# Spreading the output projection, keeping h resident and moving relays and weight loads between engines in a four-layer streaming trunk

## The chip, the cores and the metric

The kernel runs on all 8 cores of one Trainium2 chip (two dies: cores 0 to 3 and 4 to 7). Each core does the same program on its own part of the batch, so there is no traffic between cores. The time is device microseconds of the slowest core. Executions come in two states: in the fast one all cores are granted about the same clock of the tensor engine (0.961 to 0.968 in a run of the changed kernel that took 4025.31 us), in the slow one a die, at times both, has a lower clock for a part of the run (0.84 on die 0 and 0.97 on die 1 in one that took 4400.8).

Engine names in the profile: PE is the tensor engine (PEld its weight loads), DVE is VectorE, ACT is ScalarE, POOL is GpSimd, SP is SyncE, which issues most transfers. In its lines `ps` is a tile of PSUM, the memory that matmuls write to, and `arena` the kernel's buffers in on-chip memory; `hd` (the normalised h), `wq` (weights converted to bf16), `wst` (weights as given) and `yd` (the convolution's result) lie in the chip's main memory.

## The reference

Four gated layers, `x <- x + W_out(mixer(branch) * silu(z))`, and a last RMS norm. The mixers are a causal pooling, a depthwise convolution of width 31 with GLU and LayerNorm, a gated MLP over chunks of 128 positions, and the pooling again.

```python
for i in range(DEPTH):                       # 0 pool, 1 conv, 2 sgu, 3 pool
    h = rmsnorm(x, norm_g[i])                # D_MODEL 1024, D_INNER 2048
    if kind == 0:
        u, z = split(h @ pool_in_w[j]);      y, st = pool_mixer(u, ...)      # windows 2/4/8/16
    elif kind == 1:
        a, gl, z = split(h @ conv_in_w[j]);  y, st = conv_mixer(a * sigmoid(gl), ...)   # then LayerNorm, silu
    else:
        u, v, z = split(h @ sgu_in_w[j]);    y, st = sgu_mixer(u, v, ...)    # W_s @ layernorm(v), times u
    x = x + (y * silu(z)) @ out_w
return rmsnorm(x, final_g), states
```

A core has 4096 prompt positions (8 groups of 512 columns) and one small group of 128 columns (samples), nine groups in all.

## The kernel before

The kernel records operations and lets a scheduler of its own order each engine's queue by simulated times. A queue then runs in that order: in the trace of before each engine does its operations in one and the same order on all 8 cores (3551 on VectorE, 1662 transfers on SyncE), though their times differ. The program has five stages: A the first pooling layer, B the convolution's front (input products, GLU, transposition, a Toeplitz product called a fill, which reads the transposed GLU result of a channel tile, T), C its back (LayerNorm, gate, projection), D the gated MLP, E the second pooling layer.

The output projection of a group is one block: eight steps of sixteen matmuls (L696 in the profile of before). Each step is followed by a residual add on VectorE, a Square on ScalarE and, two *ticks* later, a statistic matmul that sums the squares for the next RMS norm. A tick is one product of eight matmuls or one projection step.

```python
def tick(self):
    for p in self.pend:
        p[0] -= 1
    while self.pend and self.pend[0][0] <= 0:
        self.pend.pop(0)[1]()

def sq_stat(self, xt, k, T, st):
    q = self.sqp.tile()
    self.S.add("act", lambda e: e.activation(out=q..., in_=xt[k]..., func=AF.Square), ...)
    def stat():                                        # run later, after n ticks
        self.pe(lambda e: e.matmul(st[0]..., lhsT=self.ones_d, rhs=q...), ...)
    return stat

def outproj(self, lay, g, ym, wn):
    xt = self.load_x(g, ...)                           # the group's residual, eight tiles
    for m in range(8):
        w = self.chunk(wn(m))
        ...                                            # 16 matmuls
        S.add("dve", ... op=ALU.add ...)               # residual
        S.add("sp", ... store to xs ...)
        self.later(2, self.sq_stat(xt, m, T, st))
        self.tick()
    def fin(): ...                                     # root, reciprocal, eight products, store of h
    self.later(2, fin)

def pool_layer(self, j, lay):
    ...
    for g in range(g0, NG):
        self.pool_cts(j, g, h, range(0, 2), ym)        # a channel tile: two input products, window sums
        self.pending_out()                             # the whole projection of the last group
        self.pool_cts(j, g, h, range(2, 8), ym)
        ...
    self.ulast(j); self.pending_out()
```

In the convolution's front every channel tile goes through the nine groups, forwards and backwards in turn. A tile's fills come between the next tile's products, and the first fill needs all nine parts of T.

```python
for ct in range(16):
    for i in range(NG):
        if not plan[ct * NG + i]:
            hres[g] = self.load_h(g, self.hB)          # 7 of the 9 h tiles stay, the others are loaded again
        pg = self.inproj(w, 128, h, n);  # ACT: sigmoid
        pa = self.inproj(w, 0, h, n);    # DVE: product into G
        S.add("dve", lambda e: e.transpose(T...[strided by NBLK], G...))   # L1028
        for _ in range(2 if i in (2, 4) else 1):
            if fills: fills.pop(0)()                   # 6 Toeplitz matmuls, a PSUM copy on ACT
```

In stage C the gate product `y * silu(z)` runs on GpSimd (L1154). In stage D a group has four chunks of LayerNormed v, then sixteen gating steps; the whole projection of the last group stood between the two.

## Time and profile before

Fast executions took 4175.99 and 4195.81 us; 4583.94 was slow.

I cut each core's trace at the same four events: the first GLU product (A to B), the end of the last fill (B to C), the first v matmul (C to D), the first copy of the last layer's u (D to E). The "floor" is the number of matmuls of each width (512, 136, 128 and fewer columns) by 0.2192, 0.073 and 0.06 us, the rates that the prediction derives: 49 matmuls of 512 columns in 10.74 us, twelve of 136 in 0.88, and the last an estimate from these two. I count it on the cores whose traces hold all 18681 matmuls; on two of the eight some 350 records are missing. These marks differ by up to 43 us from the windows in the prediction. Means over the 8 cores, in us:

| stage | length | floor | above the floor | PE idle |
|---|---|---|---|---|
| A | 980 | 768 | 212 | 181 |
| B | 611 | 536 | 75 | 71 |
| C | 760 | 569 | 191 | 162 |
| D | 1008 | 976 | 32 | 38 |
| E | 806 | 716 | 90 | 77 |
| sum | 4164 | 3564 | 600 | 529 |

(In D PE's matmuls ran 5 us under these rates in all, so the idle time is more than what is above the floor.)

The lines of the profile that carry this are in the prediction below. Here are only stages B and D on the slowest core with these marks; the columns are window, length, busy us of PE, PEld, DVE, ACT, POOL with instruction counts, granted clock, DMA share, GB/s:

```profile
1002.00:1609.00 607.00, 535.90 (x3252) 281.93 (x3316) 524.58 (x450) 318.69 (x566) 29.31 (x66) 0.95 0.75 206
2368.00:3373.00 1005.00, 964.24 (x5028) 467.13 (x5122) 515.63 (x849) 320.94 (x457) 0.20 (x1) 0.99 0.61 198
```

In B VectorE is nearly as full as PE (525 and 536 of 607 us); in D PE is all but gapless.

### The profile page before, as it was taken

The numbers are of one execution on the slowest core, as the hardware profiler recorded it, in microseconds if no ns is written. First come the engines' busy times: TensorE is split into PE (matmuls) and PEld (weight loads), VectorE is DVE, ScalarE is ACT, GpSimd is POOL, SyncE is SP. The second block draws the span as 40 slices with busy tenths as digits, with TensorE's granted clock in tenths as the row PEclk, the third lists the DMA queues.
The fourth block names the chain that finished last, engine by engine and source line by source line (L and its number), as shares of the span: only waits on it lengthen the run. The fifth ranks groups of instructions, "written<-read, shape, count | busy, mean of one in ns | idle before, by whom it ended". The sixth has DMA issues, their size and how long they took to land.

```text
span 4179.6 us, 58691 instructions; the slowest of 8 cores (4148.8 to 4179.6 us)
## 1 busy us (share of the span) xinstructions
PE 3614.8 (86%) x18339; PEld 1720.5 (41%) x18681; DVE 2568.2 (61%) x3551; ACT 1608.5 (38%) x2677; POOL 504.9 (12%) x887
## 2 busy tenths in 40 slices
PE   6996888884997997797886799999999989999996
PEld 2442333342444543243333444444444444444443
DVE  4855677663888995554544445555455666677775
ACT  3332333222554553565565433223333222332222
POOL 1211111111000000224223100000000011111100
PEclk9998999997999998898998899999999999999998
DMA  7655666579886668566656735666556763233224
GB/s 163 127 124 122 139 150 138 135 161 203 203 209 180 187 186 241 176 214 212 221 179 203 239 133 185 197 201 194 194 178 194 246 221 106 91 106 106 94 87 96
DMA packets 274912, 704.49 MB, mean 169 GB/s; under 512 B 53848, under 2 KB 67288, under 8 KB 261296
## 3 DMA queue, kind: packets, MB, share of 16 engines
q1 hardware_dynamic: 257584, 612.62, 45.7%
q0 software_dynamic: 17024, 88.09, 13.3%
q8 instruction: 157, 2.57, 0.3%
q14 instruction: 147, 1.20, 0.1%
HBM read 645.97 MB, written 176.26 MB: 197 GB/s over the span
## 4 chain that ended last, share of the span: by engine, by line
PE 63%; DVE 16%; DMA 8%; issue 6%; ACT 3%; POOL 2%; SPq 1%; DVEq 0%; ACTq 0%; POOLq 0%
PE ps L608 31%; PE ps L696 21%; DVE arena L833 6%; PE ps L1243 5%; DMA arena<-wq 3%; DVE arena L654 3%; DMA arena<-wst 2%; DVE arena L647 2%; DVE arena L843 2%; PE ps L638 2%; POOL arena L1154 2%; DVE arena L1146 1%; DMA yd<-arena 1%; PE ps L1067 1%; PE ps L747 1%
## 5 line engine op out<-in xcount | busy, mean ns | idle before, releaser
L608 PE MATMUL ps<-arena 128*128 128x512 bf16 (+1 forms) x10151 | 2144.7, 366 | 192.3 <-DMA arena<-wq 54.6
L608 PEld LDWEIGHTS ps<-arena 128*128 128x128 bf16 x10368 | 970.5, 99 | 1241.5 <-issue 240.6
L696 PE MATMUL ps<-arena 128*128 128x512 bf16 (+1 forms) x4526 | 1001.0, 374 | 186.3 <-POOL arena L1154 106.5
L696 PEld LDWEIGHTS ps<-arena 128*128 128x128 bf16 x4608 | 443.7, 101 | 700.1 <-issue 253.9
L700 DVE TENSOR_TENSOR arena<-ps,arena 128x512 f32<-128x512 f32 (+1 forms) x288 | 185.3, 646 | 773.2 <-PE ps L696 706.1
L833 DVE TENSOR_TENSOR arena<-arena 128x526 f32<-128x526 f32 (+4 forms) x720 | 476.1, 661 | 105.6 <-ACT arena L811 58.5
L632 ACT ACTIVATE arena<-arena 128x512 bf16<-128x512 f32 (+1 forms) x360 | 208.1, 591 | 749.9 <-DVE arena L700 716.0
L1028 DVE STREAM_TRANSPOSE arena<-arena 128x512 bf16<-128x512 bf16 (+1 forms) x144 | 334.2, 2321 | 11.1 <-DVE arena L1002 0.5
L811 ACT ACTIVATE arena<-ps 128x512 f32<-128x512 f32 x256 | 152.6, 596 | 408.4 <-DVE arena L843 190.2
L1154 POOL TENSOR_TENSOR arena<-arena 128x512 bf16<-128x512 f32 (+1 forms) x144 | 212.0, 1510 | 467.8 <-ACT arena L1148 467.8
L849 ACT ACTIVATE arena<-ps 128x512 f32<-128x512 f32 (+1 forms) x288 | 161.5, 561 | 223.7 <-PE ps L608 202.4
L647 DVE RECIPROCAL arena<-arena 128x512 f32<-128x512 f32 (+1 forms) x54 | 166.5, 3083 | 131.5 <-ACT arena L644 131.5
L858 DVE SCALAR_TENSOR_TENSOR arena<-arena 128x512 bf16<-128x512 f32 (+1 forms) x288 | 204.3, 709 | 48.7 <-DVE arena L843 40.7
L1243 PE MATMUL ps<-arena 128*128 128x512 bf16 x1035 | 228.6, 379 | 4.4 <-DMA arena<-wq 3.2
L814 POOL COPY arena<-arena 128x15 f32<-128x15 f32 x224 | 116.0, 518 | 953.4 <-ACT arena L811 953.1
L654 DVE SCALAR_TENSOR_TENSOR arena<-arena 128x512 bf16<-128x512 f32 (+3 forms) x360 | 226.7, 702 | 5.3 <-DVE arena L647 1.6
L1327 ACT ACTIVATE arena<-ps 128x512 f32<-128x512 f32 (+1 forms) x144 | 80.7, 562 | 377.2 <-PE ps L608 377.0
L809 POOL COPY arena<-arena 128x15 f32<-128x15 f32 x256 | 63.1, 247 | 1260.3 <-DMA o_sgu<-arena 864.7
L843 DVE SCALAR_TENSOR_TENSOR arena<-arena 128x512 f32<-128x512 f32 (+1 forms) x288 | 187.0, 649 | 32.7 <-DVE arena L833 0.5
L1330 DVE TENSOR_TENSOR arena<-ps,arena 128x512 f32<-128x512 f32 (+1 forms) x144 | 92.9, 645 | 171.7 <-PE ps L608 138.8
L1080 DVE STREAM_TRANSPOSE arena<-arena 128x512 f32<-128x512 f32 x144 | 146.5, 1049 | 32.6 <-DMA yd<-arena 32.5
L982 ACT ACTIVATE arena<-arena 32x512 bf16<-32x512 f32 x256 | 160.7, 628 | 13.5 <-PE ps L1067 5.2
(75 smaller groups left out, 2405.2 us busy)
## 6 DMA issues: line engine op xcount, KB each, us to landing
arena<-wq SPq DMA_DIRECT2D x474, 512.0 KB, 4.3
arena<-hd SPq DMA_DIRECT2D x70, 1024.0 KB, 8.1
arena<-wst POOLq DMA_DIRECT2D x104, 512.0 KB, 12.0
xs<-arena SPq DMA_DIRECT2D x192, 256.0 KB, 3.9
arena<-xs SPq DMA_DIRECT2D x192, 256.0 KB, 6.6
arena<-xin SPq DMA_DIRECT2D x128, 256.0 KB, 9.6
wq<-wst POOLq DMA_DIRECT2D x64, 512.0 KB, 10.7
yd<-arena SPq DMA_DIRECT2D x128, 256.0 KB, 5.3
```

Source lines behind the costliest of these rows:

```text
L608: r = e.matmul(P[:, 0:T], lhsT=W[:, k * 256 + base:k * 256 + base + 128], rhs=H[:, k * 512:k * 512 + T], start=(k == 0), stop=(k == 7))
L632: self.S.add("act", lambda e: e.activation(out=q.ap(BF16)[:, 0:T], in_=xt[k].ap()[:, 0:T], func=AF.Square), reads=[xt[k]], writes=[q], cos ...
L647: self.S.add("dve", lambda e: e.reciprocal(out=r.ap()[:, 0:T], in_=r.ap()[:, 0:T]), reads=[r], writes=[r], cost=(6.5 * T + 80) / 1000)
L654: self.S.add("dve", lambda e, k=k: e.scalar_tensor_tensor(out=(h.ap(BF16)[:, k * 512:k * 512 + T] if h is not None else xt[k].ap()[:, 0:T] ...
L696: r = e.matmul(P[:, 0:T], lhsT=W[:, k * 128:(k + 1) * 128], rhs=ym[k].ap(BF16)[:, 0:T], start=(k == 0), stop=(k == 15))
L700: S.add("dve", lambda e, t=t, m=m: e.tensor_tensor(out=xt[m].ap()[:, 0:T], in0=t.ap()[:, 0:T], in1=xt[m].ap()[:, 0:T], op=ALU.add), reads= ...
L833: return e.tensor_tensor(out=V(dst, lo, n), in0=V(src, lo, n), in1=V(src, lo - step, n), op=ALU.add)
L843: S.add("dve", lambda e, u=u, src=src, w=w: e.scalar_tensor_tensor(out=V(src, 15, nt), in0=V(src, 15, nt), scalar=1.0 / w, in1=V(u, 15, nt ...
L858: return e.scalar_tensor_tensor(out=a, in0=b, scalar=self.par[:, P_PSCALE + j * 16 + ct:P_PSCALE + j * 16 + ct + 1], in1=c, op0=ALU.mult, ...
L1028: S.add("dve", lambda e, G=G, T=T, b0=b0, nb=nb: e.transpose(T.ap(BF16)[:, 0:32 * NBLK].rearrange("p (c b) -> p b c", b=NBLK)[:, b0:b0 + n ...
L1154: S.add("pool", lambda e: e.tensor_tensor(out=o.ap(BF16)[:, 0:T], in0=y.ap()[:, 0:T], in1=z.ap()[:, 0:T], op=ALU.mult), reads=[y, z], writ ...
L1243: r = e.matmul(pv.ap()[:, 0:512], lhsT=H[:, k * 512 + c * 128:k * 512 + c * 128 + 128], rhs=w[k // 4].ap(BF16)[:, (k % 4) * 512:(k % 4) * ...
```

## The change

Its intent: take PE's waits away. The block projection becomes a generator of eight steps, pulled one at a time between the next group's input products. The front's transpositions become contiguous; the strided access moves to a second copy on ScalarE, called the relay, for one, and to the copy out of PSUM for the other. All nine h tiles stay resident, for which the second buffer of the convolution's result (Y1) goes. The gate product moves from GpSimd to VectorE. Loads of converted weights go to the Pool queue (GpSimd's), and two more sets are kept converted. The diff is shortened; `...` marks cuts.

```diff
+        yield                                   # outproj is now a generator
         for m in range(8):
+            xt += self.load_x(g, ..., [m])
 ...
             self.later(2, self.sq_stat(xt, m, T, st))
             self.tick()
+            if m < 7:
+                yield
@@ pool_layer
+            pulls = (4, 5, 7, 8, 10, 11, 13, 14)
             self.pool_cts(j, g, h, range(0, 2), ym)
-            self.pending_out()
-            self.pool_cts(j, g, h, range(2, 8), ym)
 ...
+            self.pool_cts(j, g, h, range(2, 16), ym, pulls=pulls)
+            self.add_out(lay, g, ym, wn)
-        self.ulast(j)
-        self.pending_out()
@@ pool_cts, between the z product and its silu
+            if ct in pulls:
+                self.pull()
@@ conv_front
-            if not hit and len(res) > 6:
+            if not hit and len(res) > 9:
 ...
-                S.add("dve", lambda e, ...: e.transpose(T...[strided], G...))
+                t1 = self.t1.tile()
+                S.add("dve", lambda e, ...: e.transpose(t1..., G...))
+                S.add("act", lambda e, ...: e.activation(out=T...[strided], in_=t1..., func=AF.Copy))
@@ buffers of the front
-        self.hB = Pool(S, "hB", 8192, offs(b, 8192, 3) + offs(R + 84 * kb, 8192, 4))
+        self.hB = Pool(S, "hB", 8192, ... 3) + (... 4) + offs(R + 41 * kb, 8192, 2))
-        self.Y1 = Pool(S, "Y1", 17408, offs(R + 24 * kb, 17408, 2))
+        self.Y1 = Pool(S, "Y1", 17408, offs(R + 24 * kb, 17408, 1))
@@ conv_back, gate product
-        S.add("pool", ... op=ALU.mult ...)
+        S.add("dve", ... op=ALU.mult ...)
@@ sgu_layer, after each v product
+                    if q % 2 == 1 and c >= 0:
+                        self.pull(1 if nch > 1 else 4)
-            self.pending_out()                   # stood between the chunks and the gating
@@ load_chunk
-            S.add("sp", ... dma_start(out=t, in_=wq) ..., cost=0.06)
+            S.add("pool", ... dma_start(out=t, in_=wq) ..., cost=0.55)
```

Cut: the last-row products of u moved from stage A into B, precasts (conversions of weights ahead of their use) moved, the projection in stage C pulled after channel tiles 1 to 8, pools and the scheduler's transfer model.

## The prediction

> **What bounds the kernel now.** I read the page first: TensorE (PE) is busy for 86% of the span, VectorE 61%, ScalarE 38%, GpSimd 12%, and the granted clock is below full in many slices.
>
> ```profile
> span 4179.6 us, 58691 instructions; the slowest of 8 cores (4148.8 to 4179.6 us)
> PE 3614.8 (86%) x18339; PEld 1720.5 (41%) x18681; DVE 2568.2 (61%) x3551; ACT 1608.5 (38%) x2677; POOL 504.9 (12%) x887
> ```
>
> The lines' first and last starts cut the span into the five layer stages: A first pooling layer (0 to 985), B convolution front (to 1648), C convolution back with LayerNorm (to 2357), D gating layer (to 3330), E second pooling layer. Second view, engines by stage; columns: window, length, busy us of PE, weight loads, VectorE, ScalarE, GpSimd, clock, DMA share, GB/s.
>
> ```profile
> 0.00:985.00 985.00, 786.42 (x3729) 360.22 (x3798) 626.01 (x927) 297.88 (x516) 160.65 (x396) 0.91 0.66 141
> 985.00:1648.00 663.00, 563.12 (x3383) 294.65 (x3446) 542.49 (x475) 333.43 (x590) 32.09 (x71) 0.93 0.77 206
> 1648.00:2357.00 709.00, 564.52 (x2589) 251.88 (x2641) 334.47 (x465) 420.16 (x714) 215.02 (x150) 0.89 0.61 197
> 2357.00:3330.00 973.00, 947.36 (x4808) 452.45 (x4901) 497.15 (x800) 316.99 (x442) 0.87 (x3) 0.99 0.60 195
> 3330.00:4180.00 850.00, 753.38 (x3842) 361.32 (x3903) 568.07 (x885) 240.00 (x417) 96.24 (x268) 0.95 0.36 117
> ```
>
> Third, a PE floor. The chain in order of time has unbroken runs such as 49 matmuls of 128x512 in 10.74 us, so 219 ns each; twelve 136-column matmuls in a row take 0.88 us, so some 0.07 us each; I estimate 0.06 us for 128 columns. Counted from the program, with those rates:
> - A: 3360 wide x 0.219 + 400 small x 0.06 + 4 = 764
> - B: 2048 x 0.219 + 256 x 0.06 + 1024 x 0.07 = 536
> - C: 2496 x 0.219 + 296 x 0.06 + 4 = 569
> - D: 4193 x 0.219 + 920 x 0.06 = 973
> - E: 3168 x 0.219 + 392 x 0.06 = 718
>
> Sum 3560. Above the floor: A 221, B 127, C 140, D 0, E 132, together 620 us. D is at its floor; nothing can be won there. Fourth, who PE waited for (waiter, releaser, us in total, times, longest):
>
> ```profile
> PE ps L696 <- POOL arena L1154: 106.5, 10, 18.7
> PE ps L696 <- DVE arena L858: 69.4, 23, 4.6
> PE ps L608 <- DMA arena<-wq: 54.6, 12, 22.9
> PE ps L608 <- DMA arena<-wst: 40.1, 7, 15.7
> PE ps L889 <- DMA arena<-wst: 31.9, 4, 23.1
> PE ps L1067 <- DVE arena L1028: 30.4, 10, 5.9
> ```
>
> L696 is the output projection, L608 the input matmuls, L889 the last u rows. So C waits for the gate product on GpSimd before each projection; A and E for the last gate products of the group just finished; A for weights. One middle group each of A, C and E:
>
> ```profile
> 474.00:576.00 102.00, 87.26 (x390) 39.13 (x397) 72.02 (x98) 34.12 (x54) 17.00 (x43) 0.93 0.65 145
> 1899.00:1979.00 80.00, 66.74 (x291) 29.39 (x296) 37.79 (x50) 48.57 (x77) 25.61 (x17) 0.91 0.65 210
> 3567.00:3662.00 95.00, 88.55 (x394) 39.66 (x402) 66.06 (x92) 27.86 (x45) 12.06 (x34) 0.96 0.27 95
> ```
>
> Floors per group: A and E 392 x 0.219 = 86, C 296 x 0.219 = 65. No other engine fills a group. B is the exception: VectorE 542 of 663 us, which includes both ends; between 1125 and 1196 it is 66.6 of 71. These groups carry it, and the next stage's gate product:
>
> ```profile
> L1028 DVE STREAM_TRANSPOSE arena<-arena 128x512 bf16<-128x512 bf16 (+1 forms) x144 | 334.2, 2321 | 11.1 <-DVE arena L1002 0.5
> L1154 POOL TENSOR_TENSOR arena<-arena 128x512 bf16<-128x512 f32 (+1 forms) x144 | 212.0, 1510 | 467.8 <-ACT arena L1148 467.8
> L1080 DVE STREAM_TRANSPOSE arena<-arena 128x512 f32<-128x512 f32 x144 | 146.5, 1049 | 32.6 <-DMA yd<-arena 32.5
> ```
>
> [...]
> - [...] Here the bf16 one (scattered 2-byte writes) takes 2452 ns in the median for 512 elements, the f32 one (strided reads, contiguous writes) 1077, a plain 512-element product (L1002) some 700. So the address pattern costs, not the transpose.
> - [...] ScalarE copies that write 64-byte runs (L982) take 628 ns for 512, no penalty.
> - [...] granted clock 0.99 in D without gaps, 0.77 at 904 to 985. [...]
> - [...] SP's queue waits in order, 921.3 us for L608 to free weight slots, and x and h transfers stand behind those.
>
> **The change, part by part.**
> 1. *Spread projections.* Each is cut into eight steps, put between the next group's input matmuls, when its operands are old. No matmul is added. E: of 44.1 us of L858 waits, 38 go. A: of 25.2, 20. C: waits for L1154 are 106.5 in ten; I take 85 back, not all, because the instruction order still puts step one right after the last gate products, among the variance sums. At stage ends the last small projection now overlaps the next stage's start.
> 2. *Gate product from GpSimd to VectorE.* 128 x about 0.7 us, so C's VectorE goes from 37.8 to 37.8 + 16 x 0.7 = 49 us per group, ScalarE is 48; both below PE's 65. It shortens the tail (1.5 to 0.7 us a tile); counted in 1.
> 3. *Convolution transposes.* Both made contiguous: 128 x 0.7 + 16 x 0.4 = 96 for 334, and 144 x 0.75 = 108 for 146.5, an estimate from L1002. VectorE in B: 542 - 238 - 38 = 266. ScalarE gains 144 x 0.63 = 91 for the relay (L982's rate) and some 18 on the strided PSUM copies: 333 + 109 = 442, about 73% of a 605 us stage. PE becomes the bound: 34 us per channel tile (536 / 16) for about 37 now. Idle in 1050 to 1568 is 518 - 472 = 46; I take 30 back.
> 4. *h resident* (nine buffers): wide h loads fall from 70 to 34, 36 of 1 MB fewer. DMA was not B's limit; what counts is the start, 985 to 1050, where PE is busy 35 of 65 us, waiting for h behind stores. With the first two h loaded early, 25 back. The end of B keeps its round trip through memory; 5 back.
> 5. *Weights.* First-layer z and o chunks are kept as bf16, so 40 loads change from the f32 source to the half-size copy. The queue totals price the casting queue at 13.3% of 16 engines for 88.09 MB against 45.7% for 612.62, twice per MB: 3.3 against 1.65 us per 512 KB. Saved about 40 x 1.65 = 66 us of DMA time, nearly all in A, and 21 of A's 49 conversions move later (70 us). Against it 16 stores. A's weight waits for wq and wst are 38.5 + 37.5 = 76; I take 57. The last-row matmuls of A move into B, and 25 of their 30.2 us wait vanishes. 477 weight issues at 0.543 us put some 260 us on GpSimd's queue, about the 212 it loses by part 2.
> 6. *Clock.* Fewer gaps: 12 in A, 6 in E.
>
> Sum: A 57 + 25 + 20 + 12 = 114; B 30 + 25 + 5 = 60; C 85; D 5 (weights and precasts only); E 38 + 6 + 8 (shorter weight waits at its start) = 52. Together 316. From the median 4195.81: **3880**, and since I have not counted C's clock (0.89), **3875**.
>
> **Rivals.**
> - *GpSimd's queue takes the wait over.* It is in order: weight issues that wait for a free slot hold up the history copies (L809, L814) that VectorE needs, and the reverse. For: those copies already wait 953 us on ScalarE. Against: before, 104 weight loads and 64 conversions already stood there. If so, A and E keep 60 to 80 us: 3940 to 3955.
> - *ScalarE becomes B's bound.* If strided reads cost it double, as the f32 transpose suggests, relay 1.05 and copies 0.85 us for 0.50: 333 + 151 + 176 x 0.35 = 546 of 600. B would win nothing in the steady part: 3905 to 3915.
> - *LayerNorm's chain fills C.* Mean, variance, root, the 3.2 us reciprocal and sixteen products must end before step one. If a group stays at 76: 3910.
> - *It goes better.* A's and E's groups reach 87: 3790.
> - *More slow executions,* [...] One of three runs before was 4583.94. This moves the median, not a fast run.
>
> **Range and chances.** The first three rivals together would give about 4000, the good case 3790; so 3785 to 3985. Being within 2% needs three quarters of the gain lost. Faster 0.95, same 0.04, slower 0.01.
>
> **What would show each step.** L696's waits for the gate products near zero; C's group near 70, E's near 88, A's near 91; the bf16 transpose below 0.8 us, the ScalarE relay at 0.6 to 0.7; B near 600 with PE above 90% in its middle; stage D unchanged at about 970. Wrong if PE waits appear for weights in A or E, for GpSimd copies through VectorE, or for ScalarE in B, or if the granted clock falls in D.

"The bf16 one" is the transposition of L1028. Part 6, 18 us for fewer gaps, was the author's estimate; the trace of before shows only clock and gaps side by side. PE is busy for 138 of 145 us at 60 to 205, with a granted clock of 1.00, for 79 of 113 at 256 to 369, with 0.85, and for 42 of 81 at 904 to 985, with 0.77. What a gap costs is not shown, nor why slow executions should become more.

## The result, and the profile after

The changed kernel is correct and faster: the ratio of after to before is 0.9635, 95% interval 0.9579 to 0.9690. A ratio is the mean time of one kernel's fast runs over that of the other's in the same rounds, so it isn't quite the ratio of the medians. Its three fast runs were 4024.19, 4025.31 and 4041.63 us against a median of before near 4187. That is about 153 us, half of the 316 that the prediction summed up, and outside its range of 3785 to 3985.

Three of its six first executions were slow: 4148.7, 4400.8 and 4510.33. The profiled one was among them, and it shows what the state is:

```profile
die 0 (median of its cores): 4140.3 us, clock 0.916
die 1 (median of its cores): 3996.7 us, clock 0.967
```

One die is 144 us longer at a lower clock, the other as in a fast run. On cores 0 and 1 of the slow die the granted clock is 0.81 in stage E and 0.97 or 0.96 in A; on cores 2 and 3 it is 0.81 in A and 0.98 or 0.99 in E. That two cores have it in one stage and two in another is shown only in each core's own time; what lowers the clock no run shows. The fast run below doesn't have it at all (0.98 at 2185 to 3240 us, in D, and 0.99 or 1.00 at 3243 to 3990, in E, on every core). Nothing below rests on a slow die.

So the trace of after below is that of a fast execution of the same kernel, taken again with the experiments. First its page's head, then the stages of its slowest core, with the same marks and columns as before:

```profile
span 4020.8 us, 58677 instructions; the slowest of 8 cores (3996.5 to 4020.8 us)
PE 3636.3 (90%) x18681; PEld 1698.2 (42%) x18681; DVE 2382.6 (59%) x3695; ACT 1758.8 (44%) x2839; POOL 489.9 (12%) x1188
```

```profile
0.00:888.00 888.00, 771.45 (x3676) 345.27 (x3677) 624.61 (x922) 297.37 (x510) 139.70 (x389) 0.96 0.61 157
888.00:1524.00 636.00, 559.34 (x3495) 292.21 (x3494) 273.63 (x472) 465.65 (x748) 47.16 (x100) 0.95 0.67 158
1524.00:2185.00 661.00, 586.48 (x2706) 255.32 (x2703) 413.43 (x618) 439.56 (x724) 63.28 (x120) 0.95 0.73 220
2185.00:3243.00 1058.00, 990.09 (x5123) 468.68 (x5124) 517.94 (x851) 326.12 (x460) 128.62 (x244) 0.98 0.58 175
3243.00:4021.00 778.00, 728.90 (x3687) 336.73 (x3684) 552.93 (x834) 230.09 (x399) 111.17 (x336) 0.99 0.34 112
```

A and C are about 100 us shorter, E 29. B is longer although VectorE's time there fell from 525 to 274, and D is 53 longer on this core. As means over the 8 cores, above the floor, against the prediction's sum:

| stage | length | above the floor before, after | change | predicted |
|---|---|---|---|---|
| A | 881 | 212, 128 | -84 | -114 |
| B | 640 | 75, 86 | +11 | -60 |
| C | 655 | 191, 97 | -94 | -85 |
| D | 1056 | 32, 80 | +48 | -5 |
| E | 779 | 90, 55 | -35 | -52 |
| sum | 4010 | 600, 446 | -154 | -316 |

(B's length also rose by 18 us of floor, mostly the last-row products that came from A; over the program the floor hardly changes.) What is missing is 162 us: 30 in A, 71 in B, 53 in D, 17 in E, less 9 in C.

Then who PE waits for, whole program, slowest core (waiter, releaser, total us, times, longest):

```profile
PE ps L650 <- ACT arena L644: 116.1, 88, 24.4
PE ps L1170 <- ACT arena L1164: 38.0, 21, 9.3
PE ps L620 <- DMA arena<-hd: 33.6, 4, 25.8
PE ps L1190 <- ACT arena L1185: 30.6, 59, 2.7
PE ps L1116 <- ACT arena L1066: 17.5, 9, 3.0
PE ps L1358 <- ACT arena L1328: 11.9, 7, 2.0
PE ps L713 <- DMA arena<-wq: 11.0, 4, 4.0
PE ps L620 <- ACT arena L1032: 10.8, 5, 3.3
```

The waits that the prediction listed are gone: the projection (now L713) waits 6.9 us in two waits for the gate product of the pooling layers, where it was 69.4, and no line is left of the 106.5 for GpSimd. In their place stands L650, the statistic matmul, waiting for ScalarE's Square (L644). Before, the same pair (L638 for L632) was less than half of that; core 5:

```profile
PE ps L638 <- ACT arena L632: 43.5, 19, 22.7
```

The longest one, 22.7 us, is the start of the program. No wait of this kind is in the prediction.

The groups that the change touched in the front and the gate, with their mean in ns (exact shapes; the columns are as in the page: line, engine, operation, operands, count, busy us, mean ns, idle before):

```profile
L1066 ACT ACTIVATE arena<-arena 128x512 bf16<-128x512 bf16 x128 | 136.8, 1069 | 93.1 <-DVE arena L1064 91.0
L1064 DVE STREAM_TRANSPOSE arena<-arena 128x512 bf16<-128x512 bf16 x128 | 90.3, 705 | 10.5 <-DVE arena L1037 0.5
L1205 DVE TENSOR_TENSOR arena<-arena 128x512 bf16<-128x512 f32 x128 | 86.3, 686 | 88.3 <-ACT arena L1222 84.2 <-ACT arena L1199 4.0
L1131 DVE STREAM_TRANSPOSE arena<-arena 128x512 f32<-128x512 f32 x128 | 82.2, 682 | 76.9 <-DMA yd<-arena 65.3 <-ACT arena L1122 11.3
```

The transpositions came out as predicted (705 and 682 ns for 700 and 750), the relay did not: 1069 ns for 630. And the middle groups of A, C and E that answer to the three in the prediction:

```profile
528.00:621.00 93.00, 88.13 (x402) 38.70 (x401) 72.70 (x99) 34.08 (x55) 14.74 (x43) 1.00 0.52 142
1727.00:1798.00 71.00, 65.86 (x298) 28.55 (x297) 47.90 (x67) 51.78 (x80) 6.86 (x13) 1.00 0.77 243
3491.00:3581.00 90.00, 86.69 (x397) 38.37 (x396) 65.42 (x91) 27.65 (x45) 12.65 (x39) 1.00 0.31 103
```

102 became 93, 80 became 71, 95 became 90; forecast were 91, 70 and 88.

### The profile page after: what moved, and what is told of

It is laid out like the page before. It is cut to its first block, busy times and chain, and to the rows that moved or that the text cites. A ratio compares the mean times of both kernels' runs of the same rounds, so it can differ in the third digit from the quotient of the medians.

```text
span 4147.2 us, 58677 instructions; the slowest of 8 cores (3983.1 to 4147.2 us)
## 1 busy us (share of the span) xinstructions
PE 3821.5 (92%) x18681; PEld 1755.1 (42%) x18681; DVE 2385.4 (58%) x3695; ACT 1764.8 (43%) x2839; POOL 486.0 (12%) x1188
## 4 chain that ended last, share of the span: by engine, by line
PE 68%; DVE 12%; DMA 8%; ACT 5%; issue 5%; SPq 1%; DVEq 0%; ACTq 0%; POOL 0%; POOLq 0%
PE ps L620 39%; PE ps L713 19%; PE ps L1292 5%; DVE arena L863 3%; DVE arena L666 3%; DMA yd<-arena 3%; PE ps L650 2%; DVE arena L659 2%; DMA arena<-xin 2%; DMA arena<-wq 2%; PE ps L1116 1%; DMA arena<-hd 1%; DMA arena<-yd 1%; DVE arena L873 1%; ACT arena L1328 1%
## 5 line engine op out<-in xcount | busy, mean ns | idle before, releaser
L620 PE MATMUL ps<-arena 128*128 128x512 bf16 (+1 forms) x10368 | 2320.9, 380 | 65.0 <-DMA arena<-hd 28.1
L620 PEld LDWEIGHTS ps<-arena 128*128 128x128 bf16 x10368 | 1001.0, 102 | 1200.9 <-issue 486.7
L713 PE MATMUL ps<-arena 128*128 128x512 bf16 (+1 forms) x4608 | 1038.8, 382 | 21.1 <-DMA arena<-wq 12.1
L713 PEld LDWEIGHTS ps<-arena 128*128 128x128 bf16 x4608 | 450.8, 102 | 556.7 <-issue 239.0
L863 DVE TENSOR_TENSOR arena<-arena 128x526 f32<-128x526 f32 (+4 forms) x720 | 477.0, 662 | 274.3 <-ACT arena L841 217.7
L644 ACT ACTIVATE arena<-arena 128x512 bf16<-128x512 f32 (+1 forms) x360 | 209.7, 590 | 724.0 <-DVE arena L717 679.1
L579 POOL DMA_DIRECT2D arena<-wq x477 | 252.6, 530 | 1681.1 <-PE ps L1358 456.6
L717 DVE TENSOR_TENSOR arena<-ps,arena 128x512 f32<-128x512 f32 (+1 forms) x288 | 185.5, 645 | 333.3 <-PE ps L713 317.5
L1292 PE MATMUL ps<-arena 128*128 128x512 bf16 x1056 | 261.6, 396 | 13.5 <-DMA arena<-hd 9.3
L1037 DVE TENSOR_TENSOR arena<-ps,arena 128x512 bf16<-128x512 f32 x128 | 87.9, 687 | 290.1 <-ACT arena L1032 179.0
L892 DVE SCALAR_TENSOR_TENSOR arena<-arena 128x512 bf16<-128x512 f32 (+1 forms) x288 | 204.1, 709 | 47.9 <-DVE arena L873 43.0
L650 PE MATMUL ps<-arena 128*128 128x512 bf16 (+1 forms) x360 | 134.7, 388 | 87.7 <-ACT arena L644 86.4
L1317 DVE BATCH_NORM_STATS2 arena<-arena 128x6 f32<-128x512 f32 x132 | 90.9, 693 | 206.7 <-ACT arena L1297 206.6
L873 DVE SCALAR_TENSOR_TENSOR arena<-arena 128x512 f32<-128x512 f32 (+1 forms) x288 | 187.0, 649 | 33.1 <-DVE arena L863 1.4
L1066 ACT ACTIVATE arena<-arena 128x512 bf16<-128x512 bf16 (+1 forms) x144 | 146.9, 1020 | 93.1 <-DVE arena L1064 90.9
L1292 PEld LDWEIGHTS ps<-arena 128*128 128x128 bf16 x1056 | 105.9, 101 | 142.7 <-issue 48.6
```

The costliest lines, as they stand in the source:

```text
L579: S.add("pool", lambda e: e.dma_start(out=t.ap(BF16), in_=w), reads=[("wq", name)], writes=[t], cost=0.55, nbytes=128 * 4096, dk=t)
L620: r = e.matmul(P[:, 0:T], lhsT=W[:, k * 256 + base:k * 256 + base + 128], rhs=H[:, k * 512:k * 512 + T], start=(k == 0), stop=(k == 7))
L644: self.S.add("act", lambda e: e.activation(out=q.ap(BF16)[:, 0:T], in_=xt[k].ap()[:, 0:T], func=AF.Square), reads=[xt[k]], writes=[q], cos ...
L650: self.pe(lambda e: e.matmul(st[0].ap()[:, 0:T], lhsT=self.ones_d[:, :], rhs=q.ap(BF16)[:, 0:T], start=(k == 0), stop=(k == 7)), [q], [st[ ...
L713: r = e.matmul(P[:, 0:T], lhsT=W[:, k * 128:(k + 1) * 128], rhs=ym[k].ap(BF16)[:, 0:T], start=(k == 0), stop=(k == 15))
L717: S.add("dve", lambda e, t=t, m=m: e.tensor_tensor(out=xt[m].ap()[:, 0:T], in0=t.ap()[:, 0:T], in1=xt[m].ap()[:, 0:T], op=ALU.add), reads= ...
```

## The experiments

Each edit is made to the changed kernel, and each ratio is to the kernel before. Batches of four (two in the last) ran on one chip and share their runs of before; the changed kernel itself ran again in the first batch as a yardstick. Stage lengths are means over the 8 cores of the profiled execution, which was fast where not said otherwise. "Core 5" is one core whose waits I list for all versions.

> The changed kernel once more, untouched, as the yardstick for the runs beside it. Expected: the ratio to the kernel before that was measured already, 0.9635, within 0.004, about 4,025 us in the fast state. On an undisturbed core the tensor engine should again wait some 125 us for the statistic matmuls (those that take a Square of ScalarE) and some 30 us for the relays of T.

Measured: 0.9626, interval 0.9595 to 0.9656; fast runs 4022 to 4042. The ratio agreed. L650's waits on core 5 are 117.6 us (65.7 in A, 7.9 in C, 10.2 in D and 32.5 in E), a little under the 125; the fills' waits for the relay are 18.2, not 30.

### The statistic matmul, queued later

```diff
-            self.later(2, self.sq_stat(xt, m, T, st))
+            self.later(4, self.sq_stat(xt, m, T, st))
```

> One number changed: a projection step's statistic matmul is queued four steps after its projection in place of two. Theory (the spread projection made a new wait: two steps later is now only one input product of 1.75 us, while the chain projection, residual add, Square takes about 1.9 us): the waits of the statistic matmul for ScalarE on an undisturbed core fall from about 125 us to under 50 (what is left is the first group's startup, 23 us, and the normalisation of the first layer), and the ratio falls from 0.9635 to 0.943 to 0.950, that is 55 to 85 us. Rival 1 (ScalarE is simply behind with its work in these stages, so that the tensor engine meets the same delay at its next instruction): the statistic waits fall, others rise by as much, ratio 0.960 to 0.966. Rival 2 (tensor engine is held by a lower clock, not by waits): waits fall but busy time rises by the same amount, ratio 0.960 to 0.966.

Measured: **0.9457**, interval 0.9437 to 0.9476; four fast runs of 3957 to 3961. That is the theory's range, and the two rivals fall. One digit gave 69 us in the mean core (4010.2 to 3941.5): E 35, A and B together 21, D 11, C 3. E alone, core 5, first before, then the changed kernel, then this one:

```profile
PE ps L696 <- DVE arena L858: 46.3, 17, 4.6
```

```profile
PE ps L650 <- ACT arena L644: 32.5, 27, 2.0
PE ps L713 <- DVE arena L892: 3.4, 1, 3.4
```

```profile
PE ps L650 <- ACT arena L644: 7.2, 8, 2.7
```

The change took 46.3 us of one wait away and put 32.5 of another in its place. (The waits are 25 of the 35 us that E gained here; most of the rest is PE's own busy time, 728 to 716 us.) One expectation missed: on core 5 the statistic's waits over all stages fell to 65 us, not under 50. What stays is in A (52.9 of them), where 22.2 are the start of the program and 3 to 4 us a group belong to the first layer's own input norm. There the Square itself waits for the load of x (3.46 us at 429.71), which the edit doesn't touch.

A got 45 us shorter and B 25 longer. Most of that is a shift over the mark: the long wait for h lay in front of the first GLU product and now lies behind it. But it also grew, from 29.4 us around the boundary to 36.8, since A's end came sooner and the loads of h didn't.

### Three steps in place of four

```diff
-            self.later(2, self.sq_stat(xt, m, T, st))
+            self.later(3, self.sq_stat(xt, m, T, st))
```

> The statistic matmul three steps after its projection (the change has two, an earlier run four). Theory (a threshold: the statistic must stand further behind its projection than the 1.9 us of residual add and Square; three steps are at least two input products in the pooling layers, 3.5 us): nearly the whole gain of the run with four, ratio 0.945 to 0.951, and the statistic's waits in the last stage under 10 us where the change has 30. Rival (the gain of four steps came from a different order of work that the scheduler made, not from the distance): a ratio half way or nearer to 0.9626, waits of 15 us or more in the last stage.

Measured: 0.9541, interval 0.9511 to 0.9571: half way, with D 19 and A 15 us shorter, but E as long as ever (775 us for 779; 27.0 us of statistic waits in 16). These are the numbers that I had set down for the rival, another order of work. The trace speaks for the distance all the same, and says why my threshold of 1.9 us was wrong. The changed kernel, core 5, in E; columns: start, us, engine, line, operation, operands, count, and in brackets the idle time before it and what ended it:

```profile
3484.12 3.62 PE L620 MATMUL ps<-arena 128*128 128x512 bf16 x16
...
3484.36 0.75 DVE L892 SCALAR_TENSOR_TENSOR arena<-arena 128x512 bf16<-128x512 f32 x1 [0.17 <-DVE arena L873]
3485.03 1.51 DVE L863 TENSOR_TENSOR arena<-arena 128x526 f32<-128x526 f32 x2
3486.65 0.69 DVE L873 SCALAR_TENSOR_TENSOR arena<-arena 128x512 f32<-128x512 f32 x1
3487.52 0.76 DVE L892 SCALAR_TENSOR_TENSOR arena<-arena 128x512 bf16<-128x512 f32 x1 [0.17 <-DVE arena L873]
...
3488.20 0.68 DVE L717 TENSOR_TENSOR arena<-ps,arena 128x512 f32<-128x512 f32 x1
3488.97 0.63 ACT L644 ACTIVATE arena<-arena 128x512 bf16<-128x512 f32 x1 [7.44 <-DVE arena L717]
3489.74 0.38 PE L650 MATMUL ps<-arena 128*128 128x512 bf16 x1 [2.00 <-ACT arena L644]
```

At 3484.12 the projection step is done and PE goes on with two input products. The residual add (L717) could run, but VectorE's queue has the window sums of two channel tiles (L863, L873, L892) in front of it, so it starts 4.08 us later. Add, Square and hand-over take 1.5 us more, 5.6 us in all. Two input products cover 3.6 of that, and PE waits 2.0 us. VectorE is behind because, 18 to 9 us earlier, it did the norm of the group that had just ended: a reciprocal of 3.35 us and eight products of 5.39 together. That comes once in a group of E, and one more wait of 1.3 us comes before it; elsewhere the chain is the 1.9 us that I had reckoned. With three ticks there still are only two products between the step and its statistic at that place (the wait is 3.2 us in the run with three), with four there are enough. On core 5 in E, where PE doesn't wait, a statistic starts 1.7 us after the end of its step with two ticks, 3.3 with three, and 5.2 or 6.7 with four (three products, or two and the next step); before it was 3.5. At the place shown the Square is ready only 5.5 us after the step, in the run with three 6.7. The mechanism holds, but its size was VectorE's queue and not the chain alone.

### Spreading undone in the pooling layers

```diff
-            if ct in pulls:
-                self.pull()
+            # no pull between channel tiles
-            if len(self.outq) > 1:
-                self.pull(8)
+            self.drain()              # whole projection after channel tile 1
```

> The spreading undone in the two pooling layers only: a group's projection stands whole after the second channel tile of the next group, as in the kernel before; the rest of the change kept. My prediction reckoned this part at 58 us (20 for the wait on the product's last VectorE instruction and 38 in the last stage), which by itself would give a ratio of 0.976 here. Theory (spreading took away that wait, some 75 us in all, and made a new one for the statistic of about 55 in these two stages): the waits of the projection for VectorE's product come back with 60 to 80 us, the statistic's waits in the two stages fall from about 98 to under 50 us, ratio 0.966 to 0.971.

Measured: **0.9876**, interval 0.9833 to 0.9919, worse than I expected. Undoing it costs 96 us in the mean core (A 57, E 37), so the spread is worth more here than the 58 us that the prediction credited. On core 5 the projection's waits for the gate product come back, first A, then E:

```profile
PE ps L713 <- DVE arena L891: 62.1, 18, 4.5
PE ps L713 <- DVE arena L891: 49.7, 18, 4.6
```

The kernel before had 31.1 in A and 46.3 in E. A has twice as many of them as before (18 for 9): before, PE waited 42.2 us for weights at A's input products (29.8 and 12.4), and in the changed kernel it waits for none there. My reading is that those waits had let the gate products catch up, so that with the weights in time the other wait comes out at every projection. It is inferred from the counts. In any case the savings in A can't be read off the table one by one and added.

### The relay of T on VectorE

```diff
-                S.add("act", lambda e, ...: e.activation(out=T...[strided], in_=t1..., func=AF.Copy), cost=c_act(...))
+                S.add("dve", lambda e, ...: e.tensor_copy(out=T...[strided], in_=t1...), cost=0.2 + c_tt(...))
```

> The relay of T goes back from ScalarE to VectorE (contiguous transposition and then a strided VectorE copy). Theory (the relay costs ScalarE 1.07 us where I had reckoned 0.63, so ScalarE took VectorE's place as what the convolution front waits for): the tensor engine's waits for the relay (19 us) and for the PSUM evictions of ScalarE (10 us) in that stage fall by 15 to 30 us in all, ScalarE's busy time there falls from 465 us to about 310, VectorE's rises from 274 by the length of 144 copies; ratio 0.956 to 0.960. Rival (the front stage is held by the transfers of h at its two ends and by VectorE's order of work whoever relays): ratio 0.962 to 0.967, the waits moving from ScalarE to VectorE.

Measured: 0.9607, interval 0.9588 to 0.9625, between the two expectations and not to be told from the yardstick. The front fell by 10 us (640 to 630). ScalarE's time there fell from 465 to 340, and the copy takes VectorE 603 ns where ScalarE took 1069. But the waits moved, as the rival said. Core 5, front stage, the changed kernel and this one:

```profile
PE ps L1116 <- ACT arena L1066: 18.2, 9, 3.9
PE ps L620 <- ACT arena L1032: 10.5, 6, 2.5
PE ps L620 <- DMA arena<-hd: 6.8, 3, 6.0
PE ps L1116 <- ACT arena L1032: 6.3, 5, 2.2
```

```profile
PE ps L1116 <- DVE arena L1037: 14.8, 4, 4.3
PE ps L620 <- DVE arena L1037: 12.5, 6, 3.1
PE ps L1116 <- DVE arena L1066: 9.6, 7, 1.4
```

### T's transposition as before

```diff
-                t1 = ...; transpose into t1 (DVE); relay into T (ACT)
+                S.add("dve", lambda e, ...: e.transpose(T...[strided], G...))
```

> The transposition of T as it was before (one VectorE instruction that writes T at a stride), the rest of the change kept. My prediction counted the transpositions as most of 30 us in the front stage; if that were so, this gives 20 us or more back, ratio 0.967 to 0.970. Theory (both versions wait for the latency of the chain at the tile's turn, and the chain is 2.4 us of strided transposition in the one and 0.71 and 1.07 in the other plus a change of engine): VectorE's busy time in the stage goes from 274 to some 410 us and ScalarE's from 465 to 310, and the stage changes by no more than 10 us; ratio 0.961 to 0.965.

Only one of eight executions was fast (4029.78), so there is no ratio, and the profiled one has a slow second die. On its undisturbed die the four cores have the same mean span as the yardstick's same four, 4011 and 4012 us, and the front is 641 and 643 us. VectorE has 500 us of work in it where the changed kernel has 274, ScalarE 340 for 465. So 226 us of VectorE's time were bought with 125 of ScalarE's and gained nothing. The prediction's step 3 read VectorE's 542 of 663 us (525 of 607 with the marks used here) as the front's limit; it wasn't. Before, in the changed kernel and in these last two, the longer waits of the fills lie at the turns of a tile, some 1 to 6 us each. My reading: the first fill needs all of T, and the chain from the last group's sigmoid to T is as long as the work in front of it. The next run tests it.

### The fills one group later

```diff
-                for _ in range(2 if i in (2, 4) else 1):
+                for _ in range((0, 1, 2, 2, 2, 1, 1, 1, 1)[i]):
```

> In the convolution front the first Toeplitz fill of a channel tile is queued one token group later (none after the first group of the next tile, two after the second, third and fourth, in place of one each). Theory (the front does not wait for VectorE's or ScalarE's capacity but for a latency at the turn of the tile: the first fill needs all of T, and the chain sigmoid, product, transposition, relay of the last group is as long as the work that stands before the fill, above all where the small group of 128 columns stands at the turn; the transpositions' change shortened one part of that chain and added another): the waits of the fills, about 30 us of the stage on an undisturbed core, fall under 10, the stage gets 18 to 28 us shorter, ratio 0.956 to 0.959 where the changed kernel has 0.9626. Rival (ScalarE is full in this stage, so the wait turns up at the next PSUM tile): the stage is as long as before within 6 us, ratio within 0.002 of the changed kernel's.

Measured: 0.9631, interval 0.9584 to 0.9678. No gain; the theory in this form fell, the rival held. On the undisturbed die of the profiled execution the front is 8 us shorter (635 for 643). The fills' waits for the relay, 19.4 us on core 1 of the yardstick, are down to 1.3, but ScalarE's other work takes their place. Core 1, front stage:

```profile
PE ps L620 <- ACT arena L1122: 10.6, 11, 1.1
PE ps L1116 <- ACT arena L1122: 10.5, 11, 1.7
...
PE ps L620 <- ACT arena L1032: 8.1, 10, 1.3
```

L1122 is the PSUM copy of the fills, L1032 the sigmoid: with the relays at 1069 ns, ScalarE is late with both. Each edit alone removes one of two causes and meets the other. That suggested both together.

### Gating: two projection steps kept back

```diff
-                    if q % 2 == 1 and c >= 0:
-                        self.pull(1 if nch > 1 else 4)
+                    if q % 2 == 1 and (nch == 1 or c < nch - 1):
+                        self.pull(1 if nch > 1 else 3)
 ...
+            self.pull(2)                      # in front of the gating matmuls
```

> In the gMLP layer two of the eight projection steps are moved from between the v products to after the last of them, in front of the gating matmuls, where the kernel before had the whole projection. Theory (spreading took away the work that had hidden the LayerNorm chain of the group's last chunk): the wait of the gating matmul on ScalarE's normalisation falls from 14 us to under 4, a group of this stage from 120.6 to about 119 us, ratio 0.960 to 0.962, a gain of 10 to 15 us. Rival (the 20 us that this stage lost come from the loads of weights and h in its first group): the gating wait falls but the stage is as long as before, ratio within 0.002 of the changed kernel's.

Measured: 0.9590, interval 0.9560 to 0.9620, a little better than expected. D is 18 us shorter (1056 to 1038), and the gating matmul's wait for the normalisation, 12.9 us in eight on core 5, is gone (one wait of 1.7 for another line of ScalarE, L1379, was there before the edit too). In the kernel before, the whole projection stood there and covered that chain; spreading it took the cover.

### Two edits of the front, with the statistic and the gating

```diff
  later(4), relay on VectorE, fills one group later, two steps in front of the gating: the four edits above
```

> Four edits at once: the statistic matmul queued four steps later; T relayed by VectorE; two projection steps of the gMLP layer in front of its gating matmuls; the fills of the convolution front one token group later. If the gains of the first three simply add (0.9457 for the first, 0.002 for the relay, 0.0036 for the gating), the ratio is 0.940. Theory on the front stage (its waits are a latency at the tile's turn AND ScalarE being full, so that either edit alone, as measured, only moved the wait from one to the other, while both together remove it): the front stage falls by 20 us or more against the same kernel without the two edits, and the ratio is 0.931 to 0.937. Rival (the front stage is held by something that neither touches): 0.939 to 0.943.

Measured: **0.9336**, interval 0.9261 to 0.9410, in the theory's range. Three fast runs of 3905 to 3912. Against the kernel with the statistic's edit alone, the front is 30 us shorter (664 to 635) and D 18. The interval doesn't exclude plain addition (0.940); the stage does: the relay alone gave B 10 us, the fills alone 8, together 30. (Where an edit touches neither B nor the end of A, B's length lies between 635 and 640 us, in six profiles.) What is left in the front on core 5:

```profile
PE ps L620 <- DMA arena<-hd: 37.7, 3, 25.9
PE ps L1170 <- ACT arena L1164: 23.7, 10, 9.9
PE ps L620 <- DVE arena L1037: 9.6, 4, 3.2
PE ps L1116 <- DVE arena L1037: 7.5, 5, 3.0
```

No fill waits for a relay any more; the loads of h at the beginning and the LayerNorm's first sums at the end (L1170) are what is left.

### The loads of h at the beginning of the front

```diff
-    hres[g] = self.load_h(g, self.hB if ct or i > 1 else None)
+    hres[g] = self.load_h(g, self.hB if ct or i > 1 else None, "sp" if ct else "act")
```

> The loads of h for the first channel tile of the convolution front are issued from ScalarE's queue in place of SyncE's. Theory (at the end of the pooling layer those loads stand in SyncE's queue behind stores of the residual that wait for VectorE's additions, so that they start 10 to 15 us later than their buffers come free): the tensor engine's one long wait for h at this boundary, 22.6 us on an undisturbed core, falls to between 5 and 14 us, ratio 0.959 to 0.961. Rival (the buffers come free only with the last input products[...]): the wait stays at 18 to 28 us, ratio 0.961 to 0.966.

Measured: 0.9647, interval 0.9607 to 0.9687. The rival's numbers held: the long wait is 22.1 us for 22.6, and the others for h even rose from 6.8 to 17.7. The queue isn't what holds these loads.

```diff
-            pulls = (4, 5, 7, 8, 10, 11, 13, 14)
+            pulls = () if first and g == 8 else (4, 5, 7, 8, 10, 11, 13, 14)
 ...
+            if first and g == 8:
+                self.pull(8)          # the projection of group 7, whole, after the small group
```

> At the end of the first pooling layer only: the projection of the group before last is not spread through the last, small group's input products but stands whole behind them, as cover for the five loads of h with which the convolution front begins. Theory (the loads start when the last input products free their buffers, and spreading left no work behind those products): the one wait of 22.6 us for h on an undisturbed core falls under 8 us, ratio 0.957 to 0.960. Rival (the waits of the small group for its own chain, which the spread steps hide now, take the gain back): the wait for h falls, but waits within the last group rise by 10 us or more, ratio 0.961 to 0.965.

Measured: 0.9599, interval 0.9548 to 0.9651. The single wait of 22.6 us is gone and 17.4 us in four waits are left, where there were 29.4 in all. A and B are 9 us shorter together, the upper edge of the theory. In part the cover only moves the wait, and the small group waits 10.2 us for its own copies on ScalarE where it waited 0.5, as the rival said.

### Fewer h tiles resident

```diff
-            if not hit and len(res) > 9:
+            if not hit and len(res) > 6:
```

> The plan of the convolution front keeps 7 of the 9 h tiles at a time in place of all 9, so that each channel tile loads two of them again. I expect transfers to be hidden: ratio 0.961 to 0.966, the DMA share in that stage higher by 10 points or more, waits for h in the steady part under 5 us. Rival (the resident h is worth something because the transfers were late): waits for h of 20 us or more in that stage, ratio 0.967 or higher.

Measured: **0.9718**, interval 0.9690 to 0.9745. B is 45 us longer (685 for 640), as the rival said, but not by waits for h (5.9 us in B). PE waits for ScalarE's PSUM copies and sigmoids (31.9 and 26.0 us on core 5, 2.5 and 10.5 in the yardstick), and ScalarE in turn waits for the transpositions that empty the convolution's result:

```profile
ACT arena L1066 <- DVE arena L1064: 100.4, 53, 5.6
ACT arena L1122 <- DVE arena L1131: 41.9, 9, 9.5
```

In the yardstick the second line is 0.5 us. The stores of the result land in 8.8 us for 4.8, its tiles come free later, and since the change left a single Y1 buffer, the next tile's copies stand still. That asked for one more run:

```diff
-            if not hit and len(res) > 9:
+            if not hit and len(res) > 6:
-        hB: 9 tiles, Y1: 1 buffer
+        hB: 7 tiles, Y1: 2 buffers       # both as in the kernel before
```

> As the run with seven resident h tiles, but with the two buffers for the convolution's result that the kernel before had (the room of the two h tiles). Theory (resident h and a single result buffer are a swap: reloading congests the queues, and only a single buffer turns that into a stall of ScalarE's evictions): the front stage falls from 685 us to within 10 us of the changed kernel's 640, ScalarE's wait for the result's transpositions (42 us) falls under 10 us, ratio 0.961 to 0.966, so that the resident h gives nothing by itself. Rival (the transfers themselves hold the stage): 665 us or more, ratio 0.968 or higher, and the resident h is worth over 25 us whatever the buffers.

Measured: 0.9623, interval 0.9582 to 0.9664. ScalarE's wait for L1131 is gone from its list. B is 620 us and C 670, 1290 together, where the yardstick has 1294. Resident h with one result buffer and reloaded h with two are the same in time: the change paid for the residency with a buffer that was worth as much.

### The other parts

```diff
-            S.add("pool", lambda e: e.dma_start(out=t.ap(BF16), in_=w), ..., cost=0.55, ...)
+            S.add("sp", lambda e: e.dma_start(out=t.ap(BF16), in_=w), ..., cost=0.06, ...)
```

> The loads of pre-converted weights go back from the Pool queue to SyncE's, the rest of the change kept. If the Pool queue is worth something (in SyncE's queue the loads stand behind stores that wait for arithmetic), the tensor engine's waits for weights, some 25 us in the whole kernel of which 23 in the gMLP layer, rise by 15 to 50 us, ratio 0.966 to 0.975. Rival (the Pool queue's transfers land later than SyncE's and its conversions stand in the same line): the waits for weights in the gMLP layer fall from 23 us, ratio 0.957 to 0.962.

Measured: 0.9639, interval 0.9596 to 0.9682: neither. PE's waits for weights in D are 21.6 us on core 5 where the yardstick has 22.9. Which queue loads the converted weights makes no difference that these runs show: moving all of them from one issuing queue to the other changed the ratio by less than the interval (0.9626 to 0.9639). Such a load of 512 KB landed in 4.3 us in the median from SyncE's queue (the page of before) and in 5.2 from Pool's (the page of the changed kernel's first, slow profile).

```diff
-        S.add("dve", ... gate product of stage C ...)
+        S.add("pool", ... gate product of stage C ...)
```

> The gate product of the convolution layer's second stage goes back from VectorE to Pool, its projection staying spread. It splits the 100 us that this stage gained. If the product's engine made it (the last Pool product of a group stood 11 to 18 us in front of each projection): the stage gets longer by 40 us or more, ratio 0.972 to 0.980. If the spreading made it (the product's lateness no longer matters, because the projection runs a group later): under 10 us, ratio 0.961 to 0.966. My prediction put both into one sum; I expect the spreading to have made it, with the waits for Pool's product under 10 us.

Measured: 0.9662, interval 0.9600 to 0.9724. C is 19 us longer (673 for 655), more than the 10 that I expected and far from 40. So of the stage's 105 us the engine made 19, and by the difference the spreading most of the rest. The projection doesn't wait for GpSimd even so (1.5 us); the wait sits at the LayerNorm's sums (L1170 and L1190 together 63.8 us on core 5, 37.1 in the yardstick).

```diff
+        self.drain()                 # at the end of stage C: its last, small projection
```

> The small projection that the convolution layer leaves over is done at that layer's end, where its weights lie in the chip's memory, and not in the first group of the gMLP layer. Theory (the first gMLP group is long because 4 MB of projection weights come in there beside the layer's own): the waits of the projection for weights in that stage, 11.5 us, go, the stage gets 15 to 30 us shorter and the convolution stage about 8 to 15 us longer; ratio 0.958 to 0.962. Rival (the first group waits for the layer's own weights and its h, whatever else is loaded): the stage gets shorter only by the 8 us of work that has moved, ratio 0.962 to 0.966.

Measured: 0.9600, interval 0.9573 to 0.9627. D is 25 us shorter, C 13 longer, 8 of either being work that moved, and the mean core 13 shorter: the theory. The 11.5 us that the projection waited for its weights in D are gone (6.3 of them came back in C).

### The version that puts it together

```diff
  the four edits, and the projection of group 7 as cover (e16); then also the drain at the end of stage C (e21)
```

> All edits that helped, together: statistic four steps later, T relayed by VectorE, the fills one group later, two projection steps in front of the gating matmuls, and the projection of the group before last whole behind the small group as cover for the loads of h. The first four gave 0.9336 together, the last one 10 us by itself: ratio 0.929 to 0.934, some 3,885 us. If the cover only moves the wait for h (it was 37 us in the four-edit kernel, two thirds of it late in the boundary), 0.933 to 0.937.

Measured: 0.9327, interval 0.9286 to 0.9369; fast runs 3901 to 3914. A and B are 18.6 us shorter than without the cover (1452.7 for 1471.3), D is 7 longer; in time the two can't be told apart.

> The best version so far (ratio 0.9327) with the convolution layer's small projection done in its own stage, which by itself took 13 us off the mean core. If it adds: ratio 0.929 to 0.932. If the gMLP layer's first group then waits for its own weights and h instead: 0.932 to 0.936.

Measured: 0.9328, interval 0.9285 to 0.9371; fast runs **3885, 3898 and 3900** us. D is 1007 us, where before had 1008. By the ratio it didn't add; its mean core is 8 us shorter than without the drain (3874 for 3882), within what such profiles differ by. Either of the two is about 3% under the changed kernel and 6.7% under the one before.

## Why the prediction was wrong

The direction was right, and so was stage C; the size was twice what came. Of the 162 us that are missing above the floor, the corrected version brings back 137 (from 446 to 309 above the floor), and it lands at 3885 to 3900 us. That this is close to the 3875 of the forecast doesn't bear the prediction out: it took six edits that the prediction hadn't asked for. By stage, change above the floor in us:

| stage | predicted | the change | the corrected version |
|---|---|---|---|
| A | -114 | -84 | -125 |
| B | -60 | +11 | -11 |
| C | -85 | -94 | -91 |
| D | -5 | +48 | +7 |
| E | -52 | -35 | -71 |

Step by step, as the prediction numbers them:

1. *Spread projections* is the step that failed most, at the words "No matmul is added". No matmul was, but their order changed, and with it the distance of the statistic matmul from its projection. That distance is counted in ticks, of which the step's own is the first. Before, the statistic stood behind one whole further step of sixteen matmuls, 3.5 us; between input products it stands behind one or two products of 1.75 us, against a chain of 1.9 to 5.6 us. One digit gave 69 us back. The same step missed that the block had been cover: for the normalisation in D (18 us) and, in part, for the loads of h at the end of A (9 us). The saving itself wasn't too high: undoing the spread in A and E costs 96 us, for which the sum had 58.
2. *The gate product* was counted inside C's 85. C came out at 94; the engine alone is 19 of it.
3. *Convolution transposes* failed as a whole (30 us counted, none found). The relay was mis-sized, 1069 ns for 630, so that ScalarE has 465 us in B for the 442 forecast; the prediction's second rival, "ScalarE becomes B's bound", had the relay right at 1.05, though not the PSUM copies (570 ns for 850). But the deeper error is that VectorE's share was read as the front's limit. With VectorE back at 500 us the stage is as long. The wait was a latency at the tile's turn plus, after the change, a late ScalarE; the two edits alone gave 10 and 8 us, together 30.
4. *h resident*: the 25 us for an earlier start failed: 22.6 and 6.8 us of waits for h stand where 26.5 stood. Its steady part, taken as hidden transfers, was right only as a swap: 45 us in favour of residency, the same 45 lost by halving the result's buffers.
5. *Weights*: A's waits for weights did go, from 42.2 us at the input products to none on core 5, and the last-row wait with them. But with the weights in time and the spread undone, A is only 42 us shorter than before (938 for 980, of which 15 are work that moved to B); the wait for the gate products grew from 31 to 62 us there, the statistic's from 38.5 to 55.7. The table of waits doesn't add: 57 for the weights and 20 for the projection had to come together. The Pool queue itself made no difference.
6. *Clock*: PE's busy time above the floor fell from 31 to 16 us in A and from 14 to 5 in E, 24 us where 18 were forecast, but rose in D from -5 to 13, so that the sum hardly moved (75 to 73). On the slowest cores the granted clock went from 0.91 to 0.96 in A, from 0.96 to 0.99 in E and from 0.99 to 0.98 in D.

Of the other rivals, GpSimd's queue took no wait over that the run with the loads on SyncE's would have given back, and LayerNorm's chain didn't hold C's group at 76 us (it is 71).

"D is at its floor; nothing can be won there" was true, but it left out that something could be lost there: 18 us of the gating wait, 11 of statistic waits, and late weights, of which the run with the drain gets 13 back over the whole program.

What stays open: the corrected version is 25 us above the sum of the prediction. Its front still waits for h at the beginning and for the LayerNorm's first sums at the end, and A for the first layer's own norm; none of these was tried. In C the new order of the mean and variance sums, which the change also rewrote, was not parted from the spreading. In B the second transposition and its strided PSUM copy were never undone. Nor were the kept converted weights, D's extra weight slots and the scheduler's new transfer model, which can change the order of every queue, tried by themselves. Fewer than half of the executions of some kernels were fast, so differences under half a per cent rest on the traces and not on the ratios.

## What to carry to other kernels

When a block of matmuls is cut up and scattered, look for everything whose distance was counted in that block's steps and for everything that the block covered; both become waits of another name. Don't add the lines of a table of waits: where two late things meet at one instruction, removing one uncovers the other. An engine that is busy for 86% of a stage need not be its limit: here the waits fell at the turns of the tile and not in every step, so ask at which points of the loop they fall.

## What these runs show of copies, transpositions and the clock

- ScalarE's relay of 512 bf16 elements, read with a stride of 64 bytes and written in runs of 32 bytes, took 1069 ns, VectorE's 603 for the same patterns, and a ScalarE Square with contiguous reads 625. In before, ScalarE copies that write runs of 64 bytes (L982) took 628 and the Square 627.
- A bf16 transposition of 512 elements on VectorE took 2449 ns with scattered 2-byte writes and 705 with contiguous ones.
- In the fast run that was profiled the granted clock is 0.98 at 2185 to 3240 us (D) and 0.99 or 1.00 at 3243 to 3990 (E) on all eight cores; in a slow run two cores of one die had 0.81 in stage E and its other two in stage A.
